# Two Strassen stages of a decoder block: a product of the current unit changes places with a product of the unit two ahead

## The chip, the core and the metric

The kernel runs on one core of a Trainium2 chip. The metric is the device time of one execution in microseconds, as the median of several runs. The core has a matrix engine (PE), a vector engine (DVE), a scalar engine (ACT), a general engine (POOL) and a queue engine (SP) that issues transfers; the profile calls them by these names, and PEld is PE's weight load.

## What is computed

One hybrid decoder block on x of 1024 x 1024 float32: dilated attention and retention read one RMS-normalised input through one input projection, are gated, merged and projected back, and a squared-ReLU MLP follows.

```python
xn = rmsnorm(x, norm1_g[l])
qa, ka, va, qr, kr, vr, gr, gate_a, gate_b = [xn @ wl[:, bounds[i]:bounds[i + 1]] for i in range(len(IN_SPLITS))]
...
y = jax.nn.sigmoid(gate_a) * (o_a @ w_proj_a[l]) + jax.nn.sigmoid(gate_b) * (o_r @ w_proj_b[l])
x = x + y @ w_out[l]
xn2 = rmsnorm(x, norm2_g[l])
x = x + jnp.square(jax.nn.relu(xn2 @ w_up[l])) @ w_down[l]
```

The change touches two of these products: part of the input projection (the retention's q, k, its gate gr and five eighths of the gates), called the input stage here, and xn2 @ w_up, called the up stage. Inputs have the reference's spread; w_up is 1024 x 4096.

## The kernel before

Every float32 factor is held as a pair of reduced-precision numbers, high and low (`wh`, `wl` for weights, `xh`, `xl` for data). `split` makes a pair: ACT copies the high part, DVE subtracts it for the low part. A product of two pairs is three matmuls (high by high, high by low, low by high).

The two stages use a form of Strassen's method. A unit is 256 output columns for all 1024 rows, so 2 x 2 blocks on both sides, and takes seven products N1 to N7 in place of eight. A product is one `pipe.step` of four terms, so twelve matmuls with 512 columns. The input stage has 21 units (5 of gates, 8 of q and k, 8 of gr), the up stage 16 (NU).

The seven products of a unit use three PSUM banks (`BANK`). Bank a holds N1, and then N1 + N2. When N1 is done, ACT copies it with a minus sign into a second buffer (line 387), which is bank b: N6, N7 and N4 are added there. Bank d holds N5 and then N3. Since the next product adds to the same bank, a product must wait until the copy of the one before it in that bank has been read: N2 waits for line 387, N7 for line 392 (ACT's copy of N6 as u2), N3 for line 395 (ACT's copy of N5 as u3), N4 for line 397 (DVE, u3 from N7). N3's own result is line 402 (DVE, u2). Pool `mm` has three buffers for banks a and d, pool `ms` three for b.

What becomes of the results differs. In the input stage, they are stored (through a sigmoid in the gate and gr units). In the up stage, `result` (line 1102) applies ReLU and square in two ACT steps (1111, 1112) and then forms, in three additions for N3 and one for N4 (line 1119), the seven operands of the down stage; each is split (`put_operand`, line 1124: once ACT, once DVE) into `hs`, which has four buffers, and stored to `h_d` by SP. N2's result q11 gives one operand, N7's u3 one, N3's u2 three (with q11 and u3 added), N4's q12 two.

The weights of a unit come as two raw tiles of 512 KB (`raw`), of which four fit. `add_units` (line 95) makes four pieces of them: A (for N1, N2) from the second tile, D (for N4) from half of the first, then four sums of halves in place (line 121), then B (for N6, N3) and C (for N5, N7). The steps are emitted in a fixed order, A of unit j+1, then D, B, C of unit j, and each waits until its buffer's last holder is done: A and B have two buffers, C one, D two halves. So C of unit j+1 and A of unit j+3 are emitted after N7 of unit j, D and B of unit j+2 after N4 of unit j. The second raw tile can be loaded again after B's split, the first after C's. In the profile all splits have lines 318 (ACT) and 319 (DVE); a wl of 128x512 is D, and of the wl of 128x1024 the one after the sums of line 121 is B, the one released by a raw load is A, the third C.

PE's order is the program's: `strassen_order` writes it out. The order on ACT, DVE and SP is fixed before the run by a planner, which takes, on each engine, what its own estimates show as ready, and among that, what comes first in the program. On the chip, each of these queues then runs in that order.

At the end of the up stage, some of the last unit's products start work for the down stage (lines 1184 to 1198): after its N1 the first row load, after its N2 the place `n2` for two weight pieces, later the first down products.

Of the kernel before, what the change touches and what calls it, by code (L numbers as in the profile page):

```python
# [255 lines left out]
def strassen_order(units):  # L256


    order = [(0, "N1"), (1, "N1"), (0, "N2"), (1, "N2")]
    for j in range(units):  # L260
        late = j + 3 >= units
        order += [(j, "N6"), (j, "N5")] + ([] if late else [(j + 2, "N1")]) + [(j, "N7")]
        order += [(j + 2, "N2")] if not late else [(units - 1, ("N1", "N2")[j + 3 - units])] if j + 1 < units else []
        order += [(j, "N3"), (j, "N4")]
    return order


# [1 line left out]
def hybrid_block(ctx: ExitStack, tc: tile.TileContext, a: dict, out: bass.AP):  # L269
# [465 lines left out]
    with ExitStack() as ph:  # L735
# [31 lines left out]
        for j, name in strassen_order(NIN):  # L767
            product("in", j, name, unit, operands, lambda: pu, result)
            if (j, name) == (NIN - 1, "N7"):
                start = values(first, slice(0, P), False)  # L770
# [316 lines left out]
    with ExitStack() as ph:  # L1087
# [94 lines left out]
        for j, name in strassen_order(NU):  # L1182
            product("up", j, name, unit, OP7, temps, result)
            if j == NU - 1:
                if name == "N1":
                    load_rows(0)
                if name == "N2":
                    parts = [x.rearrange("p a b -> p (a b)") for x in OP7[name]]
                    for i, part in enumerate("ab"):
                        W.places["n2" + part] = [x[:, 1024 * i:1024 * i + 1024] for x in parts]  # L1190
                    W.free(("place", "n2"))
                if name == "N5":
                    load_rows(1)
                if name == "N7":
                    down(0, "N1")
                if name == "N3":
                    load_rows(2)
                    down(0, "N2")
# [122 lines left out]
```

## Time and profile before

| what | us |
| --- | --- |
| median of 3 runs | 2305.11 (2303.64 to 2306.29) |
| the profiled execution, span | 2304.7 |
| PE busy | 2236.1 (97%) |
| DVE busy | 1339.1 (58%) |
| ACT busy | 994.1 (43%) |
| POOL busy | 103.0 (4%) |
| input stage, about | 595 to 997 of the span |
| up stage, about | 1656 to 1976 of the span |

The profile records one execution. Its span runs from the first to the last instruction; the three timed runs lie within 1.2 us of their median, and the span is 0.4 us below it. Busy times of PE are modelled at the end of each matmul, so that two neighbouring matmuls overlap in the records: one lasts 0.39 us and the next starts 0.23 us after it. Idle time is given before an instruction, with what ended it.

The views used below: windows (busy time of each engine in a stretch), waits (who waited for whom), the timeline of one engine, the chain of waits (what released what, followed back from the end), and the list of transfers with the time to landing.

### The profile page before, as it was taken

The numbers are of one execution on the slowest core, as the hardware profiler recorded it, in microseconds if no ns is written. First come the engines' busy times: TensorE is split into PE (matmuls) and PEld (weight loads), VectorE is DVE, ScalarE is ACT, GpSimd is POOL, SyncE is SP. The second block draws the span as 40 slices with busy tenths as digits, with TensorE's granted clock in tenths as the row PEclk, the third lists the DMA queues.
The fourth block names the chain that finished last, engine by engine and source line by source line (L and its number), as shares of the span: only waits on it lengthen the run. The fifth ranks groups of instructions, "written<-read, shape, count | busy, mean of one in ns | idle before, by whom it ended". The sixth has DMA issues, their size and how long they took to land.

```text
span 2304.7 us, 29956 instructions
## 1 busy us (share of the span) xinstructions
PE 2236.1 (97%) x10868; PEld 1913.1 (83%) x10868; DVE 1339.1 (58%) x2588; ACT 994.1 (43%) x2166; POOL 103.0 (4%) x148
## 2 busy tenths in 40 slices
PE   8999999999999999989999999999999999699999
PEld 7999999998888888878888778888777777488887
DVE  6444535456444445647767842454877767777774
ACT  5444434345343333435555532123666666422220
POOL 1111111110000000000000000000000000000000
PEclk9999999999999999999999999999999999899999
DMA  4313132222233333354433484553487779967665
GB/s 148 95 52 116 51 97 88 81 90 95 92 112 112 110 110 110 110 165 122 129 102 110 146 279 141 179 185 126 135 231 220 225 229 265 318 239 264 231 225 200
DMA packets 288805, 353.53 MB, mean 153 GB/s; under 512 B 14609, under 2 KB 215441, under 8 KB 288658
## 3 DMA queue, kind: packets, MB, share of 16 engines
q1 hardware_dynamic: 288658, 351.63, 48.1%
q8 instruction: 85, 1.39, 0.3%
q14 instruction: 62, 0.51, 0.1%
HBM read 229.84 MB, written 121.73 MB: 153 GB/s over the span
## 4 chain that ended last, share of the span: by engine, by line
PE 78%; DVE 8%; DMA 6%; ACT 4%; issue 3%; SPq 0%; POOL 0%; POOLq 0%; DVEq 0%; ACTq 0%
PE mm L223 52%; PE ms L223 20%; DMA raw<-in_w_up 3%; DVE hs L319 2%; PE ms L604 1%; PE ms L584 1%; ACT wh L318 1%; DVE wl L319 1%; DMA raw<-in_w_down 1%; PE tr L660 1%; DMA pa_d<-s 1%; DVE raw L121 1%; DVE xl L319 1%; DVE q L1119 1%; PE ms L597 1%
## 5 line engine op out<-in xcount | busy, mean ns | idle before, releaser
L223 PE MATMUL mm<-wh,xh 128*128 128x384 f32 (+1 forms) x1280 | 503.4, 393 | 1.2 <-DMA xh<-h_d 1.2
L223 PE MATMUL mm<-wh,xl 128*128 128x384 f32 (+1 forms) x1280 | 460.2, 360 | 5.1 <-DMA xl<-h_d 2.6
L223 PE MATMUL mm<-wl,xh 128*128 128x384 f32 (+1 forms) x1280 | 459.3, 359 | 0.0
L319 DVE TENSOR_TENSOR wl<-raw,wh 128x1024 fp32r<-128x1024 f32 (+2 forms) x274 | 296.8, 1087 | 265.5 <-ACT wh L318 263.3
L318 ACT ACTIVATE wh<-raw 128x1024 fp32r<-128x1024 f32 (+2 forms) x274 | 257.7, 949 | 285.1 <-PE mm L223 79.0
L223 PE MATMUL mm<-xh,wh 128*128 128x512 f32 x848 | 312.0, 392 | 14.8 <-ACT ms L387 14.8
L223 PE MATMUL mm<-xl,wh 128*128 128x512 f32 x848 | 310.7, 391 | 1.7 <-DVE xl L319 1.7
L223 PE MATMUL mm<-xh,wl 128*128 128x512 f32 x720 | 281.4, 391 | 0.0
L223 PEld LDWEIGHTS mm<-wh,xl 128*128 128x128 f32 x1280 | 241.3, 189 | 28.5 <-DVE xl L319 3.5
L223 PEld LDWEIGHTS mm<-wh,xh 128*128 128x128 f32 x1280 | 242.3, 189 | 22.1 <-DMA xh<-h_d 1.6
L223 PEld LDWEIGHTS mm<-wl,xh 128*128 128x128 f32 x1280 | 243.1, 190 | 19.4 <-DVE wl L319 0.4
L223 PE MATMUL ms<-xh,wh 128*128 128x512 f32 x604 | 238.5, 395 | 6.3 <-ACT u L392 3.1
L223 PE MATMUL ms<-xl,wh 128*128 128x512 f32 x604 | 235.3, 390 | 0.7 <-DVE xl L319 0.7
L223 PE MATMUL ms<-xh,wl 128*128 128x512 f32 x604 | 235.3, 390 | 0.0
L223 PEld LDWEIGHTS mm<-xh,wh 128*128 128x128 f32 x848 | 159.8, 188 | 51.9 <-ACT ms L387 19.1
L223 PEld LDWEIGHTS mm<-xl,wh 128*128 128x128 f32 x848 | 160.0, 189 | 35.1 <-DVE xl L319 2.1
L223 PEld LDWEIGHTS mm<-xh,wl 128*128 128x128 f32 x720 | 136.0, 189 | 28.6
L223 PEld LDWEIGHTS ms<-xh,wh 128*128 128x128 f32 x604 | 113.5, 188 | 32.0 <-ACT u L392 4.4
L223 PEld LDWEIGHTS ms<-xh,wl 128*128 128x128 f32 x604 | 113.4, 188 | 23.8
L223 PEld LDWEIGHTS ms<-xl,wh 128*128 128x128 f32 x604 | 113.5, 188 | 23.4 <-DVE xl L319 1.0
L591 ACT ACTIVATE pr<-s,acc 128x128 f32<-128x128 f32 (+1 forms) x96 | 43.1, 449 | 147.8 <-DVE acc L589 123.1
L1176 DVE TENSOR_TENSOR Y<-Y,ms 128x512 f32<-128x512 f32 x96 | 65.7, 684 | 62.7 <-PE ms L223 62.6
(254 smaller groups left out, 3280.1 us busy)
## 6 DMA issues: line engine op xcount, KB each, us to landing
h_d<-hs SPq DMA_DIRECT2D x112, 512.0 KB, 4.8
xh<-h_d SPq DMA_DIRECT2D x32, 896.0 KB, 6.3
xl<-h_d SPq DMA_DIRECT2D x32, 896.0 KB, 7.6
raw<-in_w_att SPq DMA_DIRECT2D x48, 384.0 KB, 4.0
raw<-in_w_up SPq DMA_DIRECT2D x32, 512.0 KB, 5.2
raw<-in_w_down SPq DMA_DIRECT2D x32, 512.0 KB, 5.9
sg_d<-sg SPq DMA_DIRECT2D x32, 256.0 KB, 2.0
raw<-in_w_rqk_q SPq DMA_DIRECT2D x16, 512.0 KB, 3.8
```

The lines of the kernel that those rows point to most:

```text
L121: self.nc.vector.tensor_tensor(x, x, y, op=OP.add)
L223: self.nc.tensor.matmul(ps, x, y, start=start, stop=stop, skip_group_check=not first)
L318: nc.scalar.activation(dst_h, src, AF.Copy)
L319: nc.vector.tensor_tensor(dst_l, src, dst_h.bitcast(F), op=OP.subtract)
L584: nc.tensor.matmul(sp[:, :n], qT[:, b * P:(b + 1) * P], kT[:, k0:k0 + n], start=True, stop=True)
L591: nc.scalar.activation(st["p"][:, :n], s[:, :n], AF.Exp, bias=acc[:, b, DH:DH + 1], accum_out=acc[:, b, DH + 1:DH + 2])
L597: nc.tensor.transpose(tp[:, j * P:(j + 1) * P], st["p"][:, j * P:(j + 1) * P], ident)
L604: nc.tensor.matmul(po[:, :DH], st["t"][:, j * P:(j + 1) * P], V[:, k0 // P + j, :], start=(j == 0), stop=(j == nk - 1))
L660: nc.tensor.transpose(pt[:, j, :], qk[:, j, :], ident)
L1119: nc.vector.tensor_tensor(held[j, x], held[j, x], held[j, y], op=OP.add)
L1176: nc.vector.tensor_tensor(Y[r][:, ns], Y[r][:, ns], ps, op=op)
```

## The change

In `strassen_order`, N3 of unit j is put directly behind N7 of the same unit, ahead of N2 of unit j+2. Before, the order of a step was N6, N5, N1 of j+2, N7, N2 of j+2, N3, N4; now it is N6, N5, N1 of j+2, N7, N3, N2 of j+2, N4. Toward the end of a stage, the same holds for the last unit's N1 and N2, which stand in that place there: its N1 comes behind N3 of the third unit from the end, its N2 behind N3 of the last but one. Both stages use this function. The down stage has an order of its own and is not touched.

```diff
@@ -260,8 +260,9 @@
     for j in range(units):
         late = j + 3 >= units
         order += [(j, "N6"), (j, "N5")] + ([] if late else [(j + 2, "N1")]) + [(j, "N7")]
+        order += [(j, "N3")]
         order += [(j + 2, "N2")] if not late else [(units - 1, ("N1", "N2")[j + 3 - units])] if j + 1 < units else []
-        order += [(j, "N3"), (j, "N4")]
+        order += [(j, "N4")]
     return order
```

## The prediction

> **What bounds the kernel now.** I read the busy table of the page first: PE is at 97%, so at most some 68 us of 2304.7 are idle anywhere, and the question is how much of that lies at the moved products. Next the windows of the two Strassen stages, the waits, and then the queues one engine at a time.
>
> ```profile
> 595.00:997.00 402.00, 402.00 (x1776) 332.85 (x1775) 187.08 (x229) 150.75 (x212) 0.00 (x0) 1.00 0.36 112
> 1700.00:1911.00 211.00, 197.07 (x843) 159.81 (x844) 149.59 (x212) 140.85 (x222) 0.00 (x0) 0.98 0.79 226
> ```
>
> Columns: window, its length, busy PE, PEld, DVE, ACT, POOL, granted clock, DMA share, GB/s. The input stage (first row) has no idle PE at all. The up stage (second row) has 13.9 us of it, with DVE at 71% and ACT at 67%: nobody is full, yet PE waits. On whom, the waits in that window say, and the chain of waits gives the pace without a wait:
>
> ```profile
> PE mm L223 <- ACT ms L387: 14.8, 10, 3.1
> ACT wh L318 <- DMA raw<-in_w_up: 30.1, 10, 4.2
> DVE wl L319 <- ACT wh L318: 38.4, 21, 4.6
> ...
> 709.50 2.72 PE ms L223 x12
> 712.22 5.44 PE mm L223 x24
> ```
>
> All of PE's waits there, ten of them, 14.8 us, are N2 waiting for L387, the ACT copy of N1's bank. A product of twelve matmuls is 2.72 us, a unit of seven 19.04. The next rows are PE's first and last such wait in the window:
>
> ```profile
> 1700.22 0.50 PE L223 MATMUL mm<-xh,wh 128*128 128x512 f32 x1 [1.05 <-ACT ms L387]
> 1721.85 0.50 PE L223 MATMUL mm<-xh,wh 128*128 128x512 f32 x1 [2.29 <-ACT ms L387]
> ...
> 1910.31 0.50 PE L223 MATMUL mm<-xh,wh 128*128 128x512 f32 x1 [1.31 <-ACT ms L387]
> ```
>
> From the first to the last are ten units: (1910.31 - 1700.22) / 10 = 21.01 us a unit, 1.97 above PE's own 19.04. Over ten units that is 19.7 us, the most that the change can bring here. Why L387 is late shows in the ACT and DVE timelines of one unit:
>
> ```profile
> 1716.98 0.57 ACT L395 ACTIVATE u<-mm 128x512 f32<-128x512 f32 x1
> 1719.65 0.63 ACT L318 ACTIVATE hs<-q 128x512 fp32r<-128x512 f32 x1 [2.10 <-DVE q L1119]
> 1720.25 1.06 ACT L318 ACTIVATE wh<-raw 128x1024 fp32r<-128x1024 f32 x1
> 1721.22 0.58 ACT L387 ACTIVATE ms<-mm 128x512 f32<-128x512 f32 x1
> ...
> 1708.86 1.23 DVE L319 TENSOR_TENSOR wl<-raw,wh 128x1024 fp32r<-128x1024 f32 x1 [4.60 <-ACT wh L318]
> 1710.00 0.69 DVE L402 TENSOR_TENSOR u<-mm,u 128x512 f32<-128x512 f32 x1
> 1710.68 0.69 DVE L319 TENSOR_TENSOR hs<-q,hs 128x512 fp32r<-128x512 f32 x1
> 1712.06 0.69 DVE L1119 TENSOR_TENSOR u<-u,u 128x512 f32<-128x512 f32 x1 [0.69 <-ACT u L1112]
> ...
> 1721.34 1.22 DVE L319 TENSOR_TENSOR wl<-raw,wh 128x1024 fp32r<-128x1024 f32 x1 [0.34 <-ACT wh L318]
> 1722.49 0.68 DVE L397 TENSOR_TENSOR u<-ms,u 128x512 f32<-128x512 f32 x1
> 1723.09 1.21 DVE L319 TENSOR_TENSOR wl<-raw,wh 128x1024 fp32r<-128x1024 f32 x1
> 1725.19 0.69 DVE L319 TENSOR_TENSOR hs<-u,hs 128x512 fp32r<-128x512 f32 x1 [0.89 <-ACT hs L318]
> 1728.36 1.23 DVE L319 TENSOR_TENSOR wl<-raw,wh 128x1024 fp32r<-128x1024 f32 x1 [2.48 <-ACT wh L318]
> 1730.79 0.68 DVE L402 TENSOR_TENSOR u<-mm,u 128x512 f32<-128x512 f32 x1
> 1732.83 0.69 DVE L1119 TENSOR_TENSOR u<-u,u 128x512 f32<-128x512 f32 x1 [1.36 <-ACT u L1112]
> ...
> 1722.59 4.65 DMA raw<-in_w_up
> 1743.25 6.02 DMA raw<-in_w_up
> ```
>
> L387 could run when N1 ends, but stands on ACT behind a split for h_d and behind wh of piece B (1720.25). And these wait for DVE, which was idle 4.60 us just before piece A's wl at 1708.86, because A's raw load had not landed. So a **loop** sets the pace and PE is not in it: wl of B ends (1722.56) and frees a raw buffer, the load runs 4.65 to 6.02 us, ACT splits A, DVE does A's wl (1728.36), then N3's chain (L402, three adds at L1119, their splits), the raw sums, and B's wl again. PE's wait at N2 is only where the loop becomes visible. That decides how I price the change.
>
> **The change, part by part.** It adds and removes nothing. In each of 21 input units and 16 up units (the last of each has no partner) N3 starts 2.72 us earlier and N2 2.72 us later; N6, N5, N1, N7 and N4 keep their places. What moves with them in the up stage: with N3, L402, two ACT steps, three adds, three splits on each of ACT and DVE, and three h_d stores on SP; with N2, two ACT steps, one split and one store. SP only exchanges stores, and the raw load is issued at 1722.59, 0.03 us after B's wl ended, so SP holds nothing up. POOL has no instruction in either window.
>
> The input stage I price at 0: PE has no idle to give, and DVE at 187.08 of 402 us is the cover. If the planner's order made N3 or N2 wait there, each wait would cost its length; N2 gets 2.72 us more room behind L387, N3 keeps a product (N7) and N1 between itself and N5's copy. In the up stage that is the tightest: L395 ends at 1717.55, and N3 would start where N7 ends, at 1721.85 - 2.29 = 1719.56, so 2.0 us cover it. PSUM: d's bank comes free a product earlier, a's a product later, and a's buffer, the third in rotation, is not asked for again until more than a unit later; 0. Weights: C and A are requested after N7 and D and B after N4, as before; 0. At the end of the up stage the last unit's N1 and N2, and with them the first row load and the place n2, come 2.72 us later, N3's buffer 2.72 us earlier; both halves are done when the pair is done, and the down weights need both in turn: 0, at worst 2.7 either way.
>
> Now the gain. The order on ACT and DVE is fixed by a planner before the run; the trace of before can't show the new one. What is safe is 2.72 us more room for L387, against a longest wait of 3.1. But if the loop still takes 21.01, PE uses that room up in 2.72 / 1.97, under two units, and waits again. The lasting gain is in what the loop drops. At present A's wl stands directly ahead of L402, with N3 ending one product after N2. With N3's result ready a product earlier, L402 can be placed ahead of A's wl, since the planner takes what is ready, in the time in which DVE now idles (4.60 and 2.48 us). The loop then loses L402's slot, about 0.60 us by the starts that follow one another (1722.49 to 1723.09 for the same kind of instruction), and the wait for its ACT steps ahead of the first add, 0.69 us in one kind of unit and 1.36 in the other (the two alternate). Together 1.29 or 1.96. I take 1.29 for both kinds: in the second kind the wait already stands behind a split of N2's result, and that filler comes later now. Against it, transfers get denser:
>
> ```profile
> raw<-in_w_up SPq DMA_DIRECT2D x32, 512.0 KB, 5.2
> raw<-in_w_rqk_q SPq DMA_DIRECT2D x16, 512.0 KB, 3.8
> ```
>
> The same size lands in 3.8 us at share 0.36 and in 5.2 at 0.79: 1.4 us per 0.43. A unit 1.1 us shorter raises the share to 0.79 x 21.01 / 19.9 = 0.83, by 0.04, so +0.15 us a load. Net 1.14 us a unit, times ten: 11.4 us. Bounds: 0 (loop unchanged) and 19.7 (PE's floor) for this part.
>
> The profiled execution has a span of 2304.7; the median of the runs shown is 2305.1, so 0.4 lies around it. **2304.7 + 0.4 - 11.4 = 2293.7 us.**
>
> One rule weighed against a row: the clock.
>
> ```profile
> 1722.00:1743.00 21.00, 21.00 (x86) 17.16 (x87) 15.12 (x22) 14.17 (x23) 0.00 (x0) 0.92 0.79 223
> ```
>
> A granted clock of 0.92 over 21 us is 1.7 us of PE time lost, right behind the wait of 2.29 us. I count it as nothing, since PE is not in the loop. The Trainium skill (TensorE: Matmul & The Clock Gate, HAM oscillation) puts the gate at idle gaps above some 3.4 us; no wait here is that long, so by the page this spell would stay after the waits went, and by the row it goes with them. The sum is the same by both as long as the loop bounds.
>
> **The rivals.** *The loop stays.* L402 remains behind A's wl. PE gains its one-time room of 2.72 us and then waits as before, perhaps at another place: 2305.1 - 2.7 = 2302.4. For it: between the two loads quoted from it, the chain of waits holds no PE step at all, so moving PE work need not touch it. The Trainium skill (TensorE: Matmul & The Clock Gate, on engine queue depths) says that ACT and DVE are strict first in, first out; the 4.60 us stall with work behind it agrees. Against it: A and L402 are neighbours in the queue and N3 moves by more than that distance.
>
> *A is planned too early, slower.* N3's adds, planned a product earlier, bring the raw sums and B's wl forward in the plan, and with them A's load. In the input stage, where B is early, DVE runs so:
>
> ```profile
> 769.71 1.23 DVE L319 TENSOR_TENSOR wl<-raw,wh 128x1024 fp32r<-128x1024 f32 x1 [4.82 <-ACT wh L318]
> 770.86 0.68 DVE L397 TENSOR_TENSOR u<-ms,u 128x512 f32<-128x512 f32 x1
> 771.46 1.22 DVE L319 TENSOR_TENSOR wl<-raw,wh 128x1024 fp32r<-128x1024 f32 x1
> ```
>
> A's wl first, then L397 and C's wl. In the up stage that order would put L397 (0.60), C's wl (1.21) and a split (0.69) behind the load instead of beside it: 2.5 us more in the loop, less the 1.36 of waiting that they fill, 1.14 a unit, 11.4 over ten: 2316.5. It decides from the point where the plan has A's load landing before N7 ends. For it: in the input stage's row the DVE waits 4.82 us and harms nobody only because there is little else. Against it: in the up stage B's wl ends (1722.56) only as L397 becomes ready, and the load behind it takes 4.65 us or more.
>
> *The change does less than it says* is the first rival.
>
> **How the numbers follow.** L402 ahead of A: 0.45, 2285 to 2300. Loop unchanged: 0.29. A too early: 0.25. The rest, 0.01, on either side. A measurement of this kernel tells about 0.2%, 4.6 us. The forecast lies beyond it, the first rival within it, the second beyond it on the other side: faster 0.46, same 0.29, slower 0.25. Range 2285 to 2317: from PE's floor to the slower case.
>
> **What would show it.** In the profile after: right, if L402 stands ahead of A's wl on DVE, the idle before A's wl shrinks, and a unit takes about 19.9 us. First rival: L387's waits gone at first but PE waiting at some other copy, and still 21 us a unit. Second: A's wl ahead of L397. If the input stage's window shows PE idle, my 0 there was wrong; if 1931 to 2020 grew, the hand-over to the down stage was.

## The result, and the profile after

The changed kernel takes 2299.32 us (median of 15 runs, 2293.55 to 2302.16) where before, on the same chip, takes 2304.26 (15 runs, 2301.01 to 2307.34). The ratio is 0.9975, with a 95% interval of 0.9968 to 0.9982: 4.9 us faster, where 11.4 were forecast. The profiled execution of the changed kernel took 2299.8 us and has a span of 2297.7. Code lines behind 262 are one higher in it (388 for 387, 393 for 392, 396 for 395, 403 for 402, 1120 for 1119).

Windows of the changed kernel, in the columns of the prediction: input stage, up stage.

```profile
595.00:997.00 402.00, 402.00 (x1775) 332.96 (x1774) 186.68 (x230) 150.94 (x212) 0.00 (x0) 1.00 0.36 112
1700.00:1911.00 211.00, 200.57 (x873) 162.52 (x872) 154.07 (x214) 136.68 (x223) 0.00 (x0) 1.00 0.81 230
```

The input stage is what it was: PE has no idle time. In the up stage PE is idle for 10.4 us, before for 13.9. Its waits in that window (who waited for whom: us in total, times, longest):

```profile
ACT wh L319 <- DMA raw<-in_w_up: 44.1, 10, 6.3
...
PE ms L223 <- ACT u L393: 10.3, 9, 2.2
...
ACT hs L319 <- DMA h_d<-hs: 7.6, 11, 1.3
```

N2 no longer waits for N1's copy at all. In its place N7 waits for line 393, the copy of N6: one wait has gone and another stands there, 10.3 us where 14.8 were. So the waits of PE say little about the time. The unit does: these are the copies of N5 on ACT in the ten units of the middle, first of before, then of the changed kernel. One row groups a line's instructions: count, shortest/mean/longest in ns, start of the first and of the last.

```profile
L395 ACT ACTIVATE u<-mm x11: 575/581/600, 1694.8 to 1904.8; 128x512 f32<-128x512 f32 x11
```

```profile
L396 ACT ACTIVATE u<-mm x11: 579/580/600, 1699.7 to 1902.7; 128x512 f32<-128x512 f32 x11
```

Eleven copies bound ten units: (1904.8 - 1694.8) / 10 = 21.0 us before, (1902.7 - 1699.7) / 10 = 20.3 after. Over all sixteen units:

```profile
L395 ACT ACTIVATE u<-mm x16: 575/580/600, 1656.8 to 1963.8; 128x512 f32<-128x512 f32 x16
```

```profile
L396 ACT ACTIVATE u<-mm x16: 579/581/600, 1657.8 to 1958.5; 128x512 f32<-128x512 f32 x16
```

307.0 us before and 300.7 after: the gain lies in the up stage. Over these fifteen units it is 0.42 us a unit; the 0.7 of the middle is too much, because N5's copies do not keep the same place in the loop. Ten laps of the loop itself, from one low part of B on DVE to the next (1699.72 to 1909.80 before, 1699.36 to 1905.71 after), average 21.01 and 20.64 us. Where in the unit it lies is read from DVE and SP. DVE of the changed kernel, from B's low part over A's to N3's subtraction:

```profile
1743.08 1.23 DVE L320 TENSOR_TENSOR wl<-raw,wh 128x1024 fp32r<-128x1024 f32 x1 [0.53 <-ACT wh L319]
1744.23 0.68 DVE L320 TENSOR_TENSOR hs<-q,hs 128x512 fp32r<-128x512 f32 x1
1744.83 0.68 DVE L398 TENSOR_TENSOR u<-ms,u 128x512 f32<-128x512 f32 x1
1745.43 1.22 DVE L320 TENSOR_TENSOR wl<-raw,wh 128x1024 fp32r<-128x1024 f32 x1
1749.70 1.23 DVE L320 TENSOR_TENSOR wl<-raw,wh 128x1024 fp32r<-128x1024 f32 x1 [3.06 <-ACT wh L319]
1750.85 0.68 DVE L403 TENSOR_TENSOR u<-mm,u 128x512 f32<-128x512 f32 x1
```

Two things are to be seen. A's low part (1749.70) still stands directly ahead of N3's subtraction (1750.85, line 403), behind an idle of 3.06 us: the step on which the forecast stood did not happen. And a split for a store (1744.23, `hs<-q`) now comes behind B's low part (1743.08); before it stood ahead. That moves a store on SP. First SP's issues before, then after:

```profile
1721.03 0.36 SPq L1129 DMA_DIRECT2D h_d<-hs  x1
1722.59 2.08 SPq L176 DMA_DIRECT2D raw<-in_w_up  x2
```

```profile
1744.34 0.35 SPq L176 DMA_DIRECT2D raw<-in_w_up  x1
1744.94 0.36 SPq L1130 DMA_DIRECT2D h_d<-hs  x1
1746.67 0.35 SPq L176 DMA_DIRECT2D raw<-in_w_up  x1
```

Before, the last store of a unit was issued 1.56 us ahead of the load of A's tile. Now that load goes first and the store follows it by 0.60 us. The chain of waits of the changed kernel has the loads with their time to landing:

```profile
1744.34 4.25 DMA raw<-in_w_up
...
1755.67 3.27 DMA h_d<-hs
...
1763.83 5.14 DMA raw<-in_w_up
```

The mean over the ten loads of A's tile from 1700 to 1912 whose landing is recorded is 5.20 us, before 5.60. I cut the loop in two legs, each a mean of ten: from the end of B's low part to the start of A's (the load's leg) 6.70 before and 6.27 after; from the end of A's to the start of the next B's (N3's leg) 11.85 and 11.91. With the two low parts, 2.45 us together, they make the lap. The leg that was forecast to shrink by 1.29 did not change, and the one that was forecast to grow by 0.15 shrank by 0.43. N3's leg has kept its length but not its content: in eight of the ten laps the chain of the changed kernel runs through the landing of a store (1755.67 above), for which ACT's next split into `hs` waits; before, it does in one of ten.

### The profile page after: what moved, and what is told of

The parts are those of the page before. It is cut to its first block, busy times and chain, and to the rows that moved or that the text cites. A ratio compares the mean times of both kernels' runs of the same rounds, so it can differ in the third digit from the quotient of the medians.

```text
span 2297.7 us, 29975 instructions
## 1 busy us (share of the span) xinstructions
PE 2236.2 (97%) x10868; PEld 1915.5 (83%) x10868; DVE 1341.9 (58%) x2588; ACT 988.0 (43%) x2166; POOL 103.0 (4%) x148
## 4 chain that ended last, share of the span: by engine, by line
PE 77%; DVE 8%; DMA 7%; ACT 4%; issue 3%; POOL 0%; SPq 0%; POOLq 0%; ACTq 0%; DVEq 0%
PE mm L223 51%; PE ms L223 20%; DMA raw<-in_w_up 3%; ACT wh L319 2%; DVE wl L320 2%; DMA h_d<-hs 1%; PE ms L605 1%; DVE hs L320 1%; PE ms L585 1%; DVE raw L121 1%; PE tr L661 1%; DVE xl L320 1%; PE ms L598 1%; PE ms L821 1%; DVE u L1120 1%
```

## The experiments

Theory: the loop of B's split, load, A's split and N3's chain sets the pace of the up stage; the change gains because the load of A's tile goes ahead of the last store; PE's order does it only by way of the planner. Rivals: PE's waits at the banks are themselves the cost; or part of the gain is made in the input stage. A unit is given by N5's copies as above. One execution is one sample of it: the same queues gave 21.0 (before) and 20.7 (e2), and 20.3 (changed) and 19.9 (e1), so a unit is good to some 0.4 us, and the ratios decide. The mean landing of A's load is no better: 5.60 (before) and 5.17 (e2), 5.20 (changed) and 4.90 (e1). So the 0.43 us by which the load's leg differs between before and the changed kernel is not clear of chance by itself.

**Each stage alone** (e1, e2)

```diff
-        order += [(j, "N3")]
-        order += [(j + 2, "N2")] if not late else ...
+        ahead = [(j + 2, "N2")] if not late else ...
+        order += [(j, "N3")] + ahead if units == 16 else ahead + [(j, "N3")]
```

(e2 with `units != 16`.)

> The exchange in the up stage alone; the input stage keeps its old order. Theory (the loop of split, load, split in the up stage sets its pace, and the whole gain is made there): ratio to before as the changed kernel's, 0.9975 with 0.9965 to 0.9985, units about 20.4 us apart where before has 21.0. Rival (part of the gain is made in the input stage, which had 402.00 of 402.00 us of TensorE): ratio nearer to 1 than 0.9985.

> The exchange in the input stage alone. Theory: within 0.1% of before (ratio 0.999 to 1.001), units of the up stage 21.0 us apart. Rival (the input stage gains): faster, ratio 0.998 to 0.999.

Measured: up stage alone 2294.07 us, ratio 0.9969 (0.9958 to 0.998). Input stage alone 0.9993 (0.9984 to 1.0002). N5's copies, up stage alone and input stage alone:

```profile
L396 ACT ACTIVATE u<-mm x11: 578/582/597, 1697.9 to 1897.1; 128x512 f32<-128x512 f32 x11
```

```profile
L396 ACT ACTIVATE u<-mm x11: 577/579/599, 1693.5 to 1900.4; 128x512 f32<-128x512 f32 x11
```

19.9 and 20.7 us a unit. The whole gain is the up stage's; what the input stage adds can't be told from none.

**The store and the load change places** (e3: before's order of products; e4: the changed order with the store put back)

e3 holds N3's last operand back until B's split has been emitted, and orders it behind:

```diff
+                if name == "N3":
+                    W.later.append(lambda x=x: put_operand(j, "N3", held[j, x]))
+                else:
+                    put_operand(j, name, held[j, x])
...
+            with tc.issue_after(W.lastB) if W.lastB else ExitStack():
+                while W.later:
+                    W.later.pop(0)()
```

e4 does the reverse in the changed kernel:

```diff
+                with self.tc.issue_after(self.hold) if self.hold and key[2] == "B" else ExitStack():
+                    self.split(h, l, self.raw[r][:, cols])
```

> Before's order of the products, but in the up stage the split of N3's last operand, which releases the last store of a unit, is put behind B's low part on VectorE, so that the load of the next tile A is issued ahead of that store. Theory (the gain is the load that goes ahead of the store; the order of products matters only through it): units about 20.4 us apart, time about 2299, ratio 0.997 to 0.9985, and TensorE still waits for the copy of N1. Rival (TensorE's own waits are the cost, and the exchange removes them): 21.0 us a unit, ratio 0.999 to 1.001.

> The changed order of products, but in the up stage B's low part stands behind the last split of N3's operand on VectorE, as it did before, so that the store is issued ahead of the load of tile A again. Theory: the gain is given back, units about 21.0 us apart, time about 2304, ratio 0.999 to 1.001. Rival (the order of products is what gains): the gain stays, about 20.4 us a unit, ratio 0.997 to 0.998.

Measured: e3, without any change of PE's order, 2294.23 us, ratio 0.9967 (0.9955 to 0.9978). e4, with the whole change of PE's order, 1.0002 (0.9994 to 1.001). First e3: N5's copies, PE's waits, SP, and a load in the chain.

```profile
L398 ACT ACTIVATE u<-mm x11: 577/579/582, 1694.9 to 1897.2; 128x512 f32<-128x512 f32 x11
```

```profile
PE mm L225 <- ACT ms L390: 9.1, 11, 1.2
```

```profile
1761.91 0.34 SPq L178 DMA_DIRECT2D raw<-in_w_up  x1
1762.52 0.36 SPq L1139 DMA_DIRECT2D h_d<-hs  x1
```

```profile
1761.91 4.33 DMA raw<-in_w_up
```

20.2 us a unit, while PE still waits for N1's copy in each (line 390 here). The load lands in 4.20 us (mean of ten); the next store ahead of it is 4.88 us away. The load's leg is 5.37 us, down by 1.33. N3's leg is 12.41, up by 0.56, since in every unit a split stands between A's low part and N3's subtraction, as it did in every second one before. The chain of waits runs through PE in five of the ten laps here, with the same legs in these as in the others. Now e4, N5's copies, SP, and DVE of the same unit:

```profile
L398 ACT ACTIVATE u<-mm x11: 576/580/584, 1694.1 to 1901.5; 128x512 f32<-128x512 f32 x11
```

```profile
1740.20 0.36 SPq L1132 DMA_DIRECT2D h_d<-hs  x1
1741.33 2.08 SPq L177 DMA_DIRECT2D raw<-in_w_up  x2
```

```profile
1744.55 0.68 DVE L405 TENSOR_TENSOR u<-mm,u 128x512 f32<-128x512 f32 x1
1747.53 1.23 DVE L321 TENSOR_TENSOR wl<-raw,wh 128x1024 fp32r<-128x1024 f32 x1 [2.30 <-ACT wh L320]
```

20.7 us a unit; the store is 1.13 us ahead of the load here (1.75 in the other units), and the load's leg is 6.53 us. e4 undid more than the store's place: in every second unit the planner also put N3's subtraction (line 405) ahead of A's low part. In these units N3's leg is 10.6 us on average and the load's 7.3, in the others 12.9 and 5.7. So e3 is the cleaner of the two. The exchange of store and load gives the gain without the exchange of products; that taking it back takes the gain away, e4 shows only together with that side effect. The likeliest reading is that the place of one store on SP is what the change was worth. No run separates the store from its split on DVE, which moves behind B's low part with it; N3's leg, where that split was, got no shorter in e3 or in the changed kernel, and the load's leg did. Why a store issued shortly before delays a load of the same queue, no run here takes apart. The Trainium skill (DMA: Bandwidth & Descriptors, Queues, rings and completion order) says that each transfer engine consumes the descriptors of one issuing queue in ring order; the landings of 5.60, 5.20 and 4.20 us, with the nearest store 1.5 to 1.75, 2.95 and 4.88 us ahead, agree with it. It is not the distance alone: in e4 the loads with the store 1.13 us ahead landed in 6.03 us, those with 1.75 in 4.60 (five each); e8 below has 1.75 us and 5.98, e10 2.96 us and 5.30, and in e11 those with 2.95 us landed in 3.73 to 4.05.

**The forecast's step by hand** (e11, e5, e9)

A's split is emitted behind N3's subtraction, by releasing buffer C there and no longer at N7 (C's split, which stands ahead of A's in the fixed order, moves with it); in e11 A's low part is ordered behind that subtraction on DVE. e5 also orders A's high part behind the square of u2 on ACT. e9 is e5 with before's order of products.

```diff
+            if tag == "up":
+                W.behind = one.ins, W.square
+                W.free((tag, j, "C"))
-        if name in ("N2", "N7", "N4", "N3"):
+        if name in ("N2", "N7", "N4", "N3") and (tag, name) != ("up", "N7"):
...
+                    for i in self.behind if key[0] == "up" and key[2] == "A" else ():
+                        if i is not None:
+                            s.enter_context(self.tc.issue_after(i))
```

> e5 without its part on ScalarE: A's low part stands behind N3's subtraction on VectorE, but A's high part stands where ScalarE's queue has it, ahead of u2's pair. This is the step as the prediction put it. As the prediction put it: units about 19.9 us, 2294 us, ratio 0.995 to 0.997. Rival 1 (ScalarE's queue, where u2's pair still stands behind the high part that waits for the load, holds N3's chain as before): units 20.2 to 21 us, ratio 0.998 to 1.001. Rival 2 (VectorE's queue alone decides): 19.04 us, ratio 0.990 to 0.992.

> The changed kernel with the premise of the forecast put in by hand: in the up stage A's high part stands behind the square of u2's pair on ScalarE and A's low part behind N3's subtraction on VectorE, so that N3's chain no longer stands behind the split of A. Forecast's step (N3's chain behind A's split is the long side of the loop): the unit goes below 20.0 us, to 19.1 to 19.9, time 2288 to 2294, ratio 0.993 to 0.996. Rival (the sums that release B's part are bound by something else, such as the number of operations in the unit on VectorE and ScalarE, or the store that a split waits for): 20.2 to 20.5 us a unit, ratio 0.997 to 0.999.

> Before's order of the products, with A's split behind u2's square on ScalarE and N3's subtraction on VectorE, as in e5. Theory now (N3's chain behind A's split is the long side of the loop; where that split stands decides, and the order of the products only by when N3 ends): nearly all of e5's gain, units 19.04 to 19.4 us, time 2281 to 2287, ratio 0.991 to 0.994. Rival (the exchange is needed as well, since N3 one product of 2.72 us later brings A's split as much later): units 19.8 to 21, ratio 0.995 to 1.0.

Measured: e11 2289.04 us, ratio 0.9954 (0.994 to 0.9968). e5 2281.24 us, ratio 0.9907 (0.9893 to 0.9922). e9 2280.37 us, 0.9912 (0.9898 to 0.9926). e11 first, N5's copies and ACT:

```profile
L401 ACT ACTIVATE u<-mm x12: 578/580/584, 1695.2 to 1913.6; 128x512 f32<-128x512 f32 x12
```

```profile
1739.82 0.63 ACT L1121 ACTIVATE u<-u 128x512 f32<-128x512 f32 x1
...
1742.29 1.06 ACT L323 ACTIVATE wh<-raw 128x1024 fp32r<-128x1024 f32 x1 [1.18 <-DMA raw<-in_w_up]
...
1757.03 0.63 ACT L1120 ACTIVATE u<-u 128x512 f32<-128x512 f32 x1
1761.74 1.06 ACT L323 ACTIVATE wh<-raw 128x1024 fp32r<-128x1024 f32 x1 [4.09 <-DMA raw<-in_w_up]
1762.71 0.61 ACT L1121 ACTIVATE u<-u 128x512 f32<-128x512 f32 x1
```

218.4 us for eleven units, 19.9 each: the forecast's size, 0.46% of 2301.11, so 10.6 us, where it had 11.4. But it is not made where the forecast had it. N3's leg is 11.89 us on average, as in the changed kernel (11.91); the load's leg is 5.57, down from 6.27: stores and loads stand in another order on SP here, and A's load lands in 4.52 us (mean of nine). ACT shows what still held N3's leg. In the second of the units shown, ReLU of u3 ends at 1757.66; its square, which needs nothing else, starts at 1762.71, because A's high part stands between them and waits 4.09 us for the load. There N3's leg is 12.85. In the first, the square (1739.82) is ahead of A's high part (1742.29), and the leg is 10.55. The two kinds alternate, but for one unit of 11.79. The step had looked at DVE alone. In e5 the high part is moved too; N5's copies and the window:

```profile
L401 ACT ACTIVATE u<-mm x12: 598/600/602, 1693.3 to 1902.7; 128x512 f32<-128x512 f32 x12
```

```profile
1700.00:1911.00 211.00, 211.00 (x933) 174.77 (x932) 167.03 (x235) 152.59 (x247) 0.00 (x0) 1.00 0.89 249
```

209.4 / 11 = 19.04 us a unit, which is PE's own time, and PE is not idle for a moment: the loop no longer binds. And on DVE:

```profile
1740.13 0.68 DVE L408 TENSOR_TENSOR u<-mm,u 128x512 f32<-128x512 f32 x1
...
1743.51 1.22 DVE L324 TENSOR_TENSOR wl<-raw,wh 128x1024 fp32r<-128x1024 f32 x1
```

N3's subtraction (1740.13) stands ahead of A's low part (1743.51), which no longer idles for the load. The last row of this part is e9's:

```profile
L400 ACT ACTIVATE u<-mm x12: 600/600/600, 1697.2 to 1906.6; 128x512 f32<-128x512 f32 x12
```

Also 19.04. With A's split in its place the exchange of products adds nothing: e5 and e9 have intervals that cover one another. Both beat before and the changed kernel, and they are the fastest versions here.

**Are PE's waits a cost?** (e7, e10)

e7 puts N6 of the next unit ahead of N4, so that its copy is done long before N7 needs it. e10 keeps that, and orders A's split ahead of N3's subtraction and of u2's pair, where the changed kernel has it.

```diff
-        order += [(j, "N6"), (j, "N5")] + ...
+        order += [(j, "N5")] + ...
...
+        order += [(j + 1, "N6")] if j + 1 < units else []
         order += [(j, "N4")]
```

> The changed kernel with N6 of the next unit put ahead of N4 of the current one, so that the copy of N6 has two products of TensorE's time more before N7 needs its bank. Theory (the waits of TensorE are where the loop shows, not what it costs): the wait for N6's copy goes and comes up at another copy or at the weights, units 20.2 to 20.5 us apart, ratio 0.997 to 0.999. Rival (the waits at the banks cost the 10.3 us that they last): units about 19.3 us apart, time about 2288, ratio 0.993 to 0.994.

> e7's order of products (N6 of the next unit ahead of N4), but with A's split put ahead of N3's subtraction on VectorE and ahead of u2's pair on ScalarE, where the changed kernel has it. Theory (e7 gained because N3's subtraction came ahead of A's low part, not because the wait for N6's copy went): the units are 20.2 to 20.6 us apart again, ratio 0.997 to 0.999. Rival (the waits at N6's copy cost what they last): 19.5 us a unit, ratio 0.992 to 0.994, as in e7.

Measured: e7 2285.76 us, ratio 0.9927 (0.9915 to 0.9939), close to the rival's number. e10 2302.3 us, 1.0005 (0.9996 to 1.0014). e7 had moved more than PE's order: with it the planner also put N3's subtraction ahead of A's low part on DVE:

```profile
1743.55 0.68 DVE L404 TENSOR_TENSOR u<-mm,u 128x512 f32<-128x512 f32 x1
1746.85 1.23 DVE L321 TENSOR_TENSOR wl<-raw,wh 128x1024 fp32r<-128x1024 f32 x1 [2.62 <-ACT wh L320]
```

It did so in all ten units, u3's pair was done ahead of A's high part on ACT, and N3's leg is 10.61 us, 1.30 shorter than in the changed kernel. So e7 alone decides nothing on PE's waits. e10 takes that part away, and with it goes the whole gain. N5's copies and PE's waits of e10:

```profile
L400 ACT ACTIVATE u<-mm x11: 577/581/600, 1694.7 to 1902.6; 128x512 f32<-128x512 f32 x11
```

```profile
PE mm L225 <- ACT ms L392: 11.2, 8, 2.2
```

N6's copy holds nobody up any more, PE waits for N1's copy instead (line 392 here), and a unit takes 20.8 us. The rival has fallen, and e9 says it more plainly: with before's order of products, and so its order in the banks, moving A's split alone left PE without any wait (211.00 of 211.00 us busy from 1700 to 1911). My theory's number was missed as well: e10 should have kept the changed kernel's 0.9975, since its load also goes ahead of the last store, and it is 0.3% slower than that. Both legs are a little longer (6.43 and 12.01 us); what in its order costs this was not tried. So a load ahead of the last store does not by itself make the gain in every order of products.

**A fifth buffer** (e6: five raw places, with A's tile loaded first; e8: five buffers for split operands; e12: only the room that both needed, a mask moved out of the constants)

```diff
-    maskT = const.tile([P, RH, P], F, name="maskT")
...
+        maskT = cp.tile([P, RH, P], F, name="maskT")
...
-            hs = temps().tile([P, 2, 512], R, name="hs", bufs=4)
+            hs = temps().tile([P, 2, 512], R, name="hs", bufs=5)
```

> The changed kernel with five places for the raw tiles of the up stage instead of four, and the two tiles of a unit loaded in the other order, so that the load of A's tile waits for a place that came free a unit earlier and not for B's part just before. Room for the fifth place comes from a mask that is moved out of the constants. Theory (the load of A's tile lies in the loop that sets the pace): the landing of the load leaves the path, units come toward the 19.04 us of TensorE, at most 19.7, time 2285 to 2292, ratio 0.992 to 0.996. Rival (TensorE's wait at the copy of N6 is a limit by itself, through the order of the products and the banks): units stay at 20.2 to 20.5 us, ratio 0.997 to 0.998.

> The changed kernel with five buffers for the split operands that are stored instead of four, room for it as with the five raw places; nothing else is changed by hand. Theory (load of A's tile, then split, then N3's chain set the pace; the stores cost only where they share the queue with that load): within 0.1% of the changed kernel, ratio 0.9965 to 0.9985. Rival (ScalarE's wait for a store, 7.6 us in 11 times in this stage, is in the loop): 0.5 us a unit less, ratio 0.994 to 0.996.

> The changed kernel with only the room that e6 and e8 made: the mask leaves the constants and is loaded into the pool of the retention stage; four raw places and four buffers for the split operands, as in the changed kernel. If that move is what e6 and e8 lost ahead of the up stage: the first copy of N5 in the up stage at about 1669 instead of 1658 us, units of 20.1 to 20.6 us as in the changed kernel, time 2308 to 2312, ratio 1.002 to 1.005. If the loss belongs to the fifth buffers: 1658 us and the changed kernel's ratio of 0.9975.

Measured: e6 0.9996 (0.9988 to 1.0005), e8 1.0052 (1.004 to 1.0064), e12 1.0031 (1.0019 to 1.0043). These missed their expectations because the room has a price, which e12 shows: against the changed kernel's 0.9975 it is 0.56%, some 13 us. Its copies of N5 in the up stage:

```profile
L394 ACT ACTIVATE u<-mm x16: 577/580/583, 1666.2 to 1963.1; 128x512 f32<-128x512 f32 x16
```

The first comes at 1666.2, not at 1657.8, so much of the price is paid ahead of that stage; on what, was not followed up. Beside e12, e6 gains 0.35% and e8 loses 0.21%. The waits of ACT for transfers in e8, from 1700 to 1911:

```profile
ACT wh L319 <- DMA raw<-in_w_up: 44.1, 10, 5.5
```

The wait for a store, 7.6 us in the changed kernel, is gone, and the time is not shorter. But the planner also put the last store ahead of the load again, 1.75 us, as in e4 (0.27% above the changed kernel), and N3's subtraction ahead of A's low part in every second unit, also as there. So what the store's landing costs in the changed kernel's loop, in whose chain it stands, e8 does not tell. In e6 it put N3's subtraction ahead of A's low part, so the fifth place was never tried by itself. Both runs are inconclusive on the buffers.

All of it in one table. Unit: from N5's copies. Legs: mean of ten; left out for e5 and e9, where PE sets the pace, and for e6, which loads A's tile in another order. The legs and 2.45 us make the lap of these ten; where it differs from the unit, by up to 0.35 us, N5's copies shifted against the loop.

| kernel | ratio to before | unit, us | load's leg, us | N3's leg, us |
| --- | --- | --- | --- | --- |
| e8, five operand buffers | 1.0052 | 21.2 | 7.16 | 11.70 |
| e12, room only | 1.0031 | 20.0 | 6.18 | 11.67 |
| before | 1 | 21.0 | 6.70 | 11.85 |
| e6, five raw places | 0.9996 | 19.8 | | |
| e2, input stage alone | 0.9993 | 20.7 | 6.40 | 11.83 |
| e4, store put back | 1.0002 | 20.7 | 6.53 | 11.76 |
| e10, N6 early, A ahead | 1.0005 | 20.8 | 6.43 | 12.01 |
| the changed kernel | 0.9975 | 20.3 | 6.27 | 11.91 |
| e1, up stage alone | 0.9969 | 19.9 | 6.00 | 11.81 |
| e3, load first, old order | 0.9967 | 20.2 | 5.37 | 12.41 |
| e11, A behind N3 on DVE | 0.9954 | 19.9 | 5.57 | 11.89 |
| e7, N6 early | 0.9927 | 19.6 | 6.58 | 10.61 |
| e9, A behind on both, old order | 0.9912 | 19.04 | | |
| e5, A behind on both | 0.9907 | 19.04 | | |

## Why the prediction was right in direction and wrong in its step

The time moved the way that was forecast and lies in the range, but not by the step that the forecast was made of. That the sign came out was luck.

*PE is not in the loop.* Right for these two kernels, but for one lap: from 1700 to 1911 the chain of waits runs through PE in one lap of ten before (1784.59) and in none after. PE's wait moved from N1's copy to N6's, and back to N1's in e10, and in e9 it went without any change of the products.

*The input stage, 0.* Right: 402.00 of 402.00 us busy, and e2.

*N3 behind N5's copy, PSUM, weights, the end of the stage, 0.* Right. From the last copy of N5 to the end of the span it is 2304.7 - 1963.8 = 340.9 us before and 2297.7 - 1958.5 = 339.2 after, 1.7 less, within the 2.7 given.

*"L402 can be placed ahead of A's wl, since the planner takes what is ready."* This is the step that failed. The planner left A's low part where it was, and N3's leg stayed (11.85 and 11.91 us). The price of the step was right: in e7, where N3's subtraction does come ahead of A's low part in every unit, N3's leg is 1.30 us shorter, where 1.29 was forecast. But DVE alone does not bring it. In e11, which does on DVE what the step said, N3's leg stays at 11.89 on average, since in every second unit A's high part on ACT holds u3's square (in the changed kernel it stands ahead of u3's pair and of u2's); its 10.6 us by the ratio came out of the load's leg, and that they are near the 11.4 is chance. e5, which moves A's split on ACT too, gains 21.4. The step read one queue, but A's split stands in two. (Between the rows 1728.36 and 1730.79 that the prediction shows, DVE has one more, a split at 1730.18; so A's low part was directly ahead of line 402 only in every second unit.) Readiness had been argued from the traced time of N3; the planner goes by its own estimates, and those I could not see. The same exchange with N6 moved as well (e7) did tip it, and e4 in every second unit.

*"SP only exchanges stores", and +0.15 us for the load.* Wrong in sign, and by e3 the likeliest source of the 4.9 us. I had counted the stores and found none held up, but I did not ask on which side of A's load each of them would be issued. The last one passed it, and the load's leg became 0.43 us shorter. N3's leg grew by 0.06, so a lap is 0.37 shorter; over the fifteen units between N5's first and last copy that is 5.6 us, beside the 6.3 by which that stretch shrank.

*At most 19.7 us.* Too low as a bound: it counted the ten units of the window, and the stage has fifteen intervals. e5's 21.4 us lie beyond it.

*"The loop stays", the first rival,* came nearer in time: its 2302.4 is 3.1 us from 2299.32, the forecast's 2293.7 is 5.6. Its sign came true as far as L387's waits go, which are gone while PE waits at another copy; the unit did not stay at 21. As ratios the two are 0.9988 and 0.9951, and both lie outside the interval. What both lacked was the place of the store. *"A is planned too early"* did not occur: A's low part (1749.70) comes behind line 398 (1744.83).

*The clock.* The up stage's granted clock rose from 0.98 to 1.00, and as PE was not in the loop, this can't be seen in the time. Waits of up to 2.2 us stayed beside it, so the prediction's row, 0.92 behind a wait of 2.29, did not tell by itself what such a wait does.

## What to carry to other kernels

Where a loop of split, load and split sets the pace, ask of each queue in it which instruction waits for the load, and what that is ready stands behind it; do this on every engine on which the piece has an instruction, here ACT as well as DVE. When a trial hits the forecast's number, look whether it made the gain in the leg that was forecast; e11 did not. When an edit moves work on a queue that issues transfers, look at which side of the critical load each store lands. A reordering that works only through a planner is a guess on the planner; an explicit order between two instructions (e5, e9) gained nearly four times as much, and did not need the reordering.

## What the runs showed of the hardware

The granted clock falls behind shorter waits of PE than I had thought, and not behind all. In e10 a wait of 2.10 us stands ahead of ten microseconds at 0.83:

```profile
1908.36 0.61 PE L225 MATMUL mm<-xh,wh 128*128 128x512 f32 x1 [2.10 <-ACT ms L392]
```

```profile
1908.00:1918.00 10.00, 9.64 (x35) 7.81 (x36) 5.42 (x7) 6.19 (x10) 0.00 (x0) 0.83 0.96 287
```

In before, a wait of 3.13 us was followed by the full clock:

```profile
1826.76 0.50 PE L223 MATMUL mm<-xh,wh 128*128 128x512 f32 x1 [3.13 <-ACT ms L387]
```

```profile
1826.00:1836.00 10.00, 9.24 (x41) 7.65 (x42) 6.03 (x7) 6.92 (x11) 0.00 (x0) 1.00 0.89 265
```

The Trainium skill (TensorE: Matmul & The Clock Gate, HAM oscillation) gives gaps above some 3.4 us as the condition; the first pair of rows doesn't agree with that, the second does.
